# An MLP's up projection by Strassen's product in place of the plain product, in a hybrid encoder kernel on one core

## The chip, the core and the metric

The kernel runs on one core of one Trainium2 chip. The metric is the time of one execution on the device in microseconds (us); the time before is the median of three runs, 2505.2 us (2502.43 to 2505.82). The profile is that of one further execution.

The engines are named as in the profile: PE is TensorE (matmuls), PEld its weight load, DVE VectorE, ACT ScalarE, POOL GpSimd, SP SyncE, which here only issues DMAs. PSUM holds the sums of the matmuls; SBUF holds everything else.

## The reference

One layer of an encoder on 1024 tokens of width 1024, in float32: a mixer (windowed attention beside a Mamba-2 scan), cross-attention, an MLP, and a final norm. The change concerns the last three lines.

```python
D_MODEL = 1024
D_FF = 4 * D_MODEL
...
        x = x + merged @ w_out[i]
        h = rmsnorm(x, norm_cross[i])
        x = x + cross_attention(h, rmsnorm(mem, norm_mem[i]), w_xq[i], w_xkv[i], w_xo[i])
        h = rmsnorm(x, norm_ffn[i])
        x = x + jnp.square(jax.nn.relu(h @ w_up[i])) @ w_down[i]
    return rmsnorm(x, norm_final)
```

## The kernel before

**Number format.** Every matmul operand is split into two parts, hi (a rounded copy, made by ACT, L66) and lo (the rest, a subtraction on POOL or DVE, L67), and a product is three matmuls, hi·hi, hi·lo and lo·hi, in one PSUM bank (mm3, L79 to L86). A weight block of 128×1024 is loaded by SP into one of two buffers `raw`, split by wload into `whi` and `wlo` (three buffers each) and then used.

**The stages.** Input projections, Mamba and windowed attention come first; they are not touched but for the buffers' names. merge_cross_phase then makes the mixer's output, adds it to x (eight tiles x1 of 128 tokens by 1024, kept in SBUF), does cross-attention for two halves of 512 tokens, h = 0 and 1, and adds its output projection in 4 units a half (xo_units, PSUM tile `xops`, 48 matmuls of 256 columns each, and four additions on DVE). Among the last units stand the norms of the MLP's input: ACT sums the squares, DVE and POOL make the factor `rr` (L118, L120), DVE scales the row tile to `xn` (L135), PE transposes it (PSUM tile `nt`), and ACT and DVE split it into the tiles `kt` (h3T).

**The MLP** (mlp_phase, from L918) runs in 16 blocks of 256 hidden columns, with up one block ahead of down. Up: two weight blocks, each giving 128 hidden columns for 1024 tokens; 8 tiles of the inner dimension × 2 halves × 3 matmuls a block, in PSUM tile `ups`; then relu on ACT (L936), a product on DVE (L938), the split on ACT and DVE (L940, L941), the result `u` staying in SBUF. Down: two blocks of w_down (`wdh`, `wdl`); for each of the 8 token tiles and 2 column halves 6 matmuls into `dps` and an addition to x1 on DVE (L964). In the last block each token tile is normed and stored as soon as it is complete.

**What sets the order.** A scheduler arranges each engine's instructions from the program's order and the pools' buffers; what stands in an engine's queue is then taken in that order, each with its waits. DMAs of weights stand in SP's queue.

## Time and profile before

| | |
|---|---|
| median of 3 runs | 2505.2 us |
| profiled execution, its own time | 2506.1 us |
| its span (first to last instruction) | 2504.2 us |
| mean granted clock of TensorE | 0.994 |
| first matmul of the output units of half 1 | 1767.2 us |
| up projection, first matmul | 1794.7 us |
| last matmul | 2495.9 us |

The busy times of the engines are shares of the span. A row of a view by operation and tile gives the engine, the operation, out<-in by the program's names, the count, and durations in ns (minimum, median, maximum); a row of the grouped view gives the busy us and the mean ns. A timeline's row gives the start and the duration in us, and in square brackets the idle time of the engine before it with what ended it. PE's matmuls overlap, so that the time between two of them, not the duration of one, says what a matmul costs.

### The profile page before, as it was taken

To read this page: it belongs to the slowest core of one execution; us is meant where nothing else is said; L and a number is where in the kernel's file an instruction comes from. 1 tells how busy PE (TensorE), PEld (TensorE's weight loads), DVE (VectorE), ACT (ScalarE), POOL (GpSimd) and SP (SyncE) were. 2 spreads that over 40 slices of the span, in tenths; PEclk is the share of its full clock that TensorE was granted. 3 is DMA by queue.
4 is the path that set the end of the run, shared out by engine and by line. 5 is a ranking of instruction groups with operands and counts; after the bars stand their busy time and mean duration, and the time that the engine had idled before them with its cause. 6 is when DMAs were issued, how large, how long until landed. Compare 5 with 4: busy or idle time off the path is not lost.

```text
span 2504.2 us, 32169 instructions
## 1 busy us (share of the span) xinstructions
PE 2434.0 (97%) x12348; PEld 2023.8 (81%) x12348; DVE 1284.3 (51%) x2033; ACT 1025.3 (41%) x2114; POOL 935.5 (37%) x808
## 2 busy tenths in 40 slices
PE   7899999999999999999999999999999999999998
PEld 6688887878878788777777878888988888888887
DVE  5747656576665753665553343235544334343435
ACT  5436455463544643666772332235422121212112
POOL 5334526354363542454444344134331221213120
PEclk9999999999999999999999999999999999999999
DMA  6213223142232322111144453321221110101111
GB/s 224 92 55 116 70 83 114 59 131 60 93 101 68 118 64 72 45 49 37 48 141 154 171 189 127 144 76 51 76 76 43 49 53 34 68 34 62 39 34 67
DMA packets 135912, 212.19 MB, mean 85 GB/s; under 512 B 9680, under 2 KB 84560, under 8 KB 135760
## 3 DMA queue, kind: packets, MB, share of 16 engines
q1 hardware_dynamic: 64864, 171.34, 19.9%
q10 hardware_dynamic: 70896, 38.81, 5.5%
q8 instruction: 97, 1.59, 0.3%
q14 instruction: 55, 0.45, 0.1%
HBM read 183.63 MB, written 26.48 MB: 84 GB/s over the span
## 4 chain that ended last, share of the span: by engine, by line
PE 68%; DVE 12%; POOL 7%; ACT 6%; issue 4%; DMA 2%; SPq 0%; POOLq 0%; ACTq 0%; DVEq 0%
PE ups L81 5%; PE ups L86 5%; PE ups L85 5%; PE dps L86 4%; PE dps L85 4%; PE dps L81 4%; PE mps L85 3%; PE mps L86 3%; PE mps L81 3%; PE zp L86 2%; PE zp L85 2%; PE zp L81 2%; PE st L454 2%; POOL wlo L67 2%; DVE cx L342 2%
## 5 line engine op out<-in xcount | busy, mean ns | idle before, releaser
L67 POOL TENSOR_TENSOR wlo<-raw,whi 128x1024 fp32r<-128x1024 f32 x170 | 412.7, 2429 | 447.5 <-ACT whi L66 412.5
L66 ACT ACTIVATE whi<-raw 128x1024 fp32r<-128x1024 f32 x172 | 181.8, 1057 | 362.4 <-PE mps L85 118.5
L964 DVE TENSOR_TENSOR x<-x,dps 128x512 f32<-128x512 f32 x256 | 175.7, 687 | 124.7 <-PE dps L86 123.0
L67 POOL TENSOR_TENSOR wdl<-raw,wdh 128x1024 fp32r<-128x1024 f32 x32 | 76.0, 2396 | 423.2 <-ACT wdh L66 423.2
L81 PE MATMUL cps<-kt,whi 128*128 128x512 f32 x512 | 217.4, 425 | 8.8 <-DVE cx L342 8.8
L86 PE MATMUL cps<-kt,wlo 128*128 128x512 f32 x512 | 201.5, 394 | 0.0
L85 PE MATMUL cps<-kt,whi 128*128 128x512 f32 x512 | 200.8, 392 | 0.0
L81 PE MATMUL ups<-kt,whi 128*128 128x512 f32 x512 | 199.7, 390 | 0.0
L85 PE MATMUL ups<-kt,whi 128*128 128x512 f32 x512 | 199.4, 389 | 0.0
L86 PE MATMUL ups<-kt,wlo 128*128 128x512 f32 x512 | 199.2, 389 | 0.0
L81 PE MATMUL dps<-wdh,u 128*128 128x512 f32 x512 | 199.2, 389 | 0.0
L85 PE MATMUL dps<-wdl,u 128*128 128x512 f32 x512 | 199.2, 389 | 0.0
L86 PE MATMUL dps<-wdh,u 128*128 128x512 f32 x512 | 199.2, 389 | 0.0
L938 DVE TENSOR_TENSOR u<-ups,ru 128x512 f32<-128x512 f32 x64 | 44.2, 690 | 256.4 <-ACT ru L936 254.6
L66 ACT ACTIVATE wdh<-raw 128x1024 fp32r<-128x1024 f32 x32 | 32.3, 1053 | 229.9 <-PE dps L86 229.7
L81 PEld LDWEIGHTS cps<-kt,whi 128*128 128x128 f32 x512 | 97.5, 190 | 34.8 <-issue 16.1
L85 PEld LDWEIGHTS cps<-kt,whi 128*128 128x128 f32 x512 | 97.3, 190 | 26.3 <-issue 7.3
L468 POOL TENSOR_TENSOR cb_t<-prev,dec 128x256 f32<-128x256 f32 x48 | 32.7, 681 | 223.7 <-ACT prev L462 221.2
L86 PEld LDWEIGHTS cps<-kt,wlo 128*128 128x128 f32 x512 | 96.9, 189 | 21.0
L81 PEld LDWEIGHTS ups<-kt,whi 128*128 128x128 f32 x512 | 96.1, 188 | 20.5 <-DVE u L938 0.4
L85 PEld LDWEIGHTS ups<-kt,whi 128*128 128x128 f32 x512 | 96.1, 188 | 20.0 <-DVE kt L144 0.2
L81 PEld LDWEIGHTS dps<-wdh,u 128*128 128x128 f32 x512 | 96.1, 188 | 19.9
(312 smaller groups left out, 6527.4 us busy)
## 6 DMA issues: line engine op xcount, KB each, us to landing
rows<-d_cs ACTq DMA_DIRECT2D x128, 256.0 KB, 3.8
raw<-in_wssd_dram SPq DMA_DIRECT2D x48, 512.0 KB, 3.3
raw<-in_wsb_dram SPq DMA_DIRECT2D x32, 512.0 KB, 3.2
raw<-in_wup_dram SPq DMA_DIRECT2D x32, 512.0 KB, 3.1
raw<-in_wdn_dram SPq DMA_DIRECT2D x32, 512.0 KB, 3.2
x<-in_x_dram SPq DMA_DIRECT2D x16, 512.0 KB, 7.3
raw<-in_wg_dram SPq DMA_DIRECT2D x16, 512.0 KB, 3.8
d_y<-yts SPq DMA_DIRECT2D x32, 256.0 KB, 2.3
```

Source lines behind the costliest of these rows:

```text
L66: nc.scalar.activation(hi, raw, AF.Copy)
L67: (eng or nc.gpsimd).tensor_tensor(lo, raw, hi.bitcast(F32), ALU.subtract)
L81: i = mm(out, l[0], r[0], start=first, stop=False)
L85: mm(out, l[0], r[1], start=False, stop=False)
L86: mm(out, l[1], r[0], start=False, stop=last)
L342: V.scalar_tensor_tensor(acc[:, :S - o], ps[:, o:], cw(k), acc[:, :S - o], ALU.mult, ALU.add)
L454: PE.matmul(st[:, lo:hi], q.btok[:, c], xs.rearrange("p d h q -> p (d h q)")[:, lo:hi], start=True, stop=True)
L468: G.tensor_tensor(heads(t), heads(prev[:, c, 1]), decay(q, 1, c), ALU.mult)
L938: V.tensor_tensor(u2, pv, r, ALU.mult)
L964: V.tensor_tensor(xh, xh, ps, ALU.add)
```

## The change

Up is split in pairs of blocks, and each pair is computed by Strassen's product (in Winograd's form): with the inputs as a 2×2 matrix of halves (a11, a12 for the first 512 tokens, the two halves of the inner dimension; a21, a22 for the last), and a pair's weights as a 2×2 matrix b11, b12, b21, b22 of 512 columns each (two weight blocks), 7 products of 12 matmuls replace 8. Sums of the inputs are made once (`Up.sums`: s1 to s4 and a22, after the transposes of the last four norms), sums of the weights for each pair (`weights`: four differences on DVE, and seven operands `wop`, hi on ACT and lo on POOL, L1073 and L1074; six buffers `wop`, now shared with wload, and `raw` still two).

Products 1 and 2 need only a11 and a12, not the sums. For pairs 0 to 7 they are made **ahead**, between the output units of half 1 and the sums, and the results (x = product 1, and c11) stored in DRAM. Then come pairs 8 to 15 in full, and pairs 0 to 7 with the other five products and x loaded again. All results go to DRAM (`d_u`), and down runs after up, in 8 blocks of twelve matmuls per addition (L1215), loading u and w_down blocks; the first block is loaded under the last three pairs. The x1 tiles of the first half are parked in DRAM (`d_x`) during up and loaded again (`xl`) at down's start. The output units of half 1 are done in two passes (two token tiles each), so their weights are loaded and split twice. PE's order is the program's own in up and down.

```diff
 def wload(kx, src, n=1024, hi=None, lo=None, eng=None):
     if hi is None:
-        hi = kx.wp.tile([P, 1024], F32R, tag="whi", bufs=kx.w_bufs, name="whi")[:, :n]
-        lo = kx.wp.tile([P, 1024], F32R, tag="wlo", bufs=kx.w_bufs, name="wlo")[:, :n]
+        hi = kx.wp.tile([P, 1024], F32R, tag="wop", bufs=6, name="whi")[:, :n]
+        lo = kx.wp.tile([P, 1024], F32R, tag="wop", bufs=6, name="wlo")[:, :n]
     split_in(kx, src, hi, lo, eng)
     return hi, lo
...
+        kx.h3 = act_tiles(kx)
+        for i in range(2):
+            norm(0, i, g_ffn, [kx.h3])
+        for i in range(2, 4):
             values(i, pend[4 + i], oks[1])
-        kx.h3T = [act_tiles(kx)]
-        for i in range(4):
-            xo_units(1, oks[1], i)
...
-def mlp_phase(kx, ins, out):
...
+def xo_units(kx, ins, h, ok, c, js=range(4)):
...
+def up_phase(kx, ins, dr, ok, grow, x1_low):
...
+        for c in range(4):
+            xo_units(kx, ins, 1, ok, c, (0, 1))
+            park(c)
+            if c in (1, 2):
+                norm_split(kx, xns[c - 1], [a11, a12], (c + 1) * P)
+        x1_low.close()
+        with tc.tile_pool(name="tp", bufs=1, side="right", reuse_waits="tile") as tp:
+            up = Up(kx, ins, dr, mp, tp, {"a11": a11, "a12": a12}, grow)
+            xns = [rows(4), rows(5)]
+            up.ahead((0,))
+            xo_units(kx, ins, 1, ok, 0, (2, 3))
+            up.sums(0, xns[0])
+            xo_units(kx, ins, 1, ok, 1, (2, 3))
+            up.ahead((1,))
+            up.sums(1, xns[1])
+            for c in range(2, 4):
+                xo_units(kx, ins, 1, ok, c, (2, 3))
+            xns = [rows(6), rows(7)]
+            up.ahead((2, 3))
+            up.sums(2, xns[0])
+            up.ahead((4, 5))
+            up.sums(3, xns[1])
+            up.ahead((6, 7))
+            order = [b for b in range(16) if b not in up.early] + sorted(up.early)
+            w = up.weights(order[0])
+            for n, b in enumerate(order):
+                nxt = up.weights(order[n + 1]) if n < 15 else None
+                if n == 13:
+                    us = down_us(kx)
+                    for j in range(4):
+                        raw = mp.tile([P, D], F32, tag="ld", bufs=2, name="uraw")
+                        split_u(kx, dr, us, j, raw)
+                if n == 14:
+                    wd = [down_wd(kx)]
+                    for j in range(2):
+                        raw = mp.tile([P, D], F32, tag="ld", bufs=2, name="draw")
+                        split_wd(kx, ins, wd[0][2 * j:2 * j + 2], j, raw, nc.vector)
+                up.quad(b, w)
+                w = nxt
+            wd.append(down_wd(kx))
+            for j in range(2, 4):
+                raw = mp.tile([P, D], F32, tag="ld", bufs=2, name="draw")
+                split_wd(kx, ins, wd[1][2 * j - 4:2 * j - 2], j, raw, nc.vector if j == 2 else nc.gpsimd)
+    return us, wd[0] + wd[1]
+
+
...
+def split_u(kx, dr, us, m, raw):
+    nc = kx.nc
...
+        t = us[2 * (m % 4) + h]
+        rh = raw[:, h * 512:(h + 1) * 512]
+        nc.scalar.activation(t[:, 0], rh, AF.Copy)
+        nc.vector.tensor_tensor(t[:, 1], rh, t[:, 0].bitcast(F32), ALU.subtract)
+
...
+    nc.scalar.activation(hl[0], raw, AF.Copy)
...
+
...
+        s3["s2"] = kx.mp.tile([P, 4, 2, 512], F32R, tag="kt", bufs=4, name="kt")
+        for key in ("s1", "s3", "s4", "a22"):
+            s3[key] = mp.tile([P, 4, 2, 512], F32R, tag=key, bufs=1, name=key)
+        self.early = set()
...
+        return self.tp.tile([P, 512], F32, tag="t2", bufs=8, name=name)
...
+        def put(key, src, eng):
+            hi, lo = hl(key)
+            A.activation(hi, src, AF.Copy)
+            eng.tensor_tensor(lo, src, hi.bitcast(F32), ALU.subtract)
+
+        f1, f2, f3, f4 = (self.t2(n).rearrange("p (k c) -> p k c", k=4) for n in ("f1", "f2", "f3", "f4"))
+        h11, l11 = (x.bitcast(F32) for x in hl("a11"))
+        h12, l12 = (x.bitcast(F32) for x in hl("a12"))
+        A.activation(f1, pv[0], AF.Copy)
+        V.tensor_tensor(f3, h11, pv[0], ALU.subtract)
+        V.tensor_tensor(f1, f1, pv[1], ALU.add)
+        put("s1", f1, G)
+        V.tensor_tensor(f3, f3, l11, ALU.add)
+        V.tensor_tensor(f2, pv[1], f3, ALU.subtract)
+        put("s2", f2, G)
+        put("a22", pv[1], V)
+        put("s3", f3, G)
+        V.tensor_tensor(f4, h12, f2, ALU.subtract)
+        V.tensor_tensor(f4, f4, l12, ALU.add)
+        put("s4", f4, G)
+
+    def put(self, src):
+        t = self.kx.wp.tile([P, 2, 512], F32R, tag="wop", bufs=6, name="wop")
+        self.kx.nc.scalar.activation(t[:, 0], src, AF.Copy)
+        self.kx.nc.gpsimd.tensor_tensor(t[:, 1], src, t[:, 0].bitcast(F32), ALU.subtract)
+        return t
+
...
+    def weights(self, b):
+        V = self.kx.nc.vector
+        put = self.put
+        b11, b21 = self.raw(2 * b)
+        b12, b22 = self.raw(2 * b + 1)
+        ts = [self.t2(f"w{n}") for n in range(2)]
+        o = {} if b in self.early else {1: put(b11), 2: put(b21)}
+        V.tensor_tensor(ts[0], b12, b11, ALU.subtract)
+        V.tensor_tensor(ts[1], b22, ts[0], ALU.subtract)
+        o[6] = put(ts[1])
+        o[5] = put(ts[0])
+        V.tensor_tensor(ts[0], b22, b12, ALU.subtract)
+        o[7] = put(ts[0])
+        o[3] = put(b22)
+        V.tensor_tensor(ts[1], b21, ts[1], ALU.subtract)
+        o[4] = put(ts[1])
+        return o
+
+    def product(self, ps, w, n, start):
...
+        for k in range(4):
+            ks = slice(k * P, (k + 1) * P)
+            for m, (i, j) in enumerate(((0, 0), (0, 1), (1, 0))):
+                self.kx.nc.tensor.matmul(ps, w[:, i, ks], act[:, k, j], start=start and k == 0 and m == 0,
+                                         stop=k == 3 and m == 2, skip_group_check=True)
+
+    def square(self, c, b, j, h):
+        self.kx.nc.vector.scalar_tensor_tensor(c, c, 0.0, c, ALU.max, ALU.mult)
+        self.kx.nc.sync.dma_start(self.dr.u[2 * b + j][:, h * 512:(h + 1) * 512], c)
...
+    def ahead(self, bs):
+
+
+        kx = self.kx
+        for b in bs:
+            w = self.early_weights(b)
+            cd = kx.pg.tile([P, S], F32, tag="g", name="pcd")
+            x, c11 = self.t2("x"), self.t2("c11")
+            self.product(cd[:, :512], w[1], 1, True)
+            kx.nc.scalar.activation(x, cd[:, :512], AF.Copy)
+            kx.nc.sync.dma_start(self.dr.u[2 * b + 1][:, :512], x)
+            self.product(cd[:, 512:], w[2], 2, True)
+            kx.nc.vector.tensor_tensor(c11, x, cd[:, 512:], ALU.add)
+            self.square(c11, b, 0, 0)
+            self.early.add(b)
...
+    def quad(self, b, w):
+        kx = self.kx
+        V, A = kx.nc.vector, kx.nc.scalar
...
+        pb = kx.pp.tile([P, 512], F32, tag="p", name="pb")
+        cd = kx.pg.tile([P, S], F32, tag="g", name="pcd")
+        pc, pd = cd[:, :512], cd[:, 512:]
+        c12 = self.t2("c12")
+        if early:
+            x = self.t2("x")
+            kx.nc.sync.dma_start(x, self.dr.u[2 * b + 1][:, :512])
+        else:
+            c11 = self.t2("c11")
+            self.product(pb, w[1], 1, True)
+            A.activation(c11, pb, AF.Copy)
+            self.product(pd, w[2], 2, True)
+            V.tensor_tensor(c11, c11, pd, ALU.add)
+            self.square(c11, b, 0, 0)
+
+        def whole(dst, ps):
+            if early:
+                V.tensor_tensor(dst, x, ps, ALU.add)
+            else:
+                A.activation(dst, ps, AF.Copy)
+
+        self.product(pb, w[6], 6, early)
+        whole(c12, pb)
+        self.product(pc, w[5], 5, True)
+        c22, c21 = self.t2("c22"), self.t2("c21")
+        whole(c22, pc)
+        self.product(pb, w[7], 7, False)
+        V.tensor_tensor(c22, c22, pb, ALU.add)
+        self.square(c22, b, 1, 1)
+        self.product(pc, w[3], 3, False)
+        V.tensor_tensor(c12, c12, pc, ALU.add)
+        self.square(c12, b, 1, 0)
+        self.product(pb, w[4], 4, False)
+        if early:
+            V.tensor_tensor(c21, x, pb, ALU.add)
+            A.activation(c21, c21, AF.Relu)
+        else:
+            A.activation(c21, pb, AF.Relu)
+        A.activation(c21, c21, AF.Square)
+        kx.nc.sync.dma_start(self.dr.u[2 * b][:, 512:], c21)
...
+def down_phase(kx, ins, dr, first, out):
...
+        NB = 8
+
...
+                us, wd = down_us(kx), down_wd(kx) + down_wd(kx)
+            for j in range(4):
+                m = 4 * b + j
+                split_u(kx, dr, us, m, fp.tile([P, D], F32, tag="uraw", bufs=2, name="uraw"))
+                split_wd(kx, ins, wd[2 * j:2 * j + 2], m, kx.wp.tile([P, D], F32, tag="raw", bufs=2, name="raw"), G)
...
+        for t in range(4):
+            kx.x1[t] = xp.tile([P, D], F32, tag="xl", bufs=4, name="xl")
+            nc.sync.dma_start(kx.x1[t], dr.x1[t])
+        nxt = first
...
-                    for j in range(2):
-                        mm3(kx, ps, kt_pair(us[j][t // 4], slice((t % 4) * P, (t % 4) * P + P)),
-                            (wd[j][0][:, cs], wd[j][1][:, cs]), j == 0, j == 1)
+                    for j in range(4):
+                        mm3(kx, ps, kt_pair(us[2 * j + t // 4], slice((t % 4) * P, (t % 4) * P + P)),
+                            (wd[2 * j][:, cs], wd[2 * j + 1][:, cs]), j == 0, j == 3)
                     xh = kx.x1[t][:, cs]
                     V.tensor_tensor(xh, xh, ps, ALU.add)
```

POOL's queue at the end of the output units and the first sums. Before, it holds factors of norms (`rr`) and one lo part of a weight block (`wlo`) per block:

```order
L67 TENSOR_TENSOR wlo_16287<-raw_16288,whi_16286 128x1024
L120 TENSOR_TENSOR rr_16172<-rv_16170,mhalf_133 128x1
L67 TENSOR_TENSOR wlo_16356<-raw_16357,whi_16355 128x1024
L120 TENSOR_TENSOR rr_16196<-rv_16194,mhalf_133 128x1
L120 TENSOR_TENSOR rr_16218<-rv_16216,mhalf_133 128x1
```

In the changed kernel the same place of POOL's queue holds also the operands of the products made ahead (`wop`) and the lo parts of the sums (s1, s3, `kt` for s2, s4):

```order
L1074 TENSOR_TENSOR wop_16292<-raw_16290,wop_16292 128x512
L1074 TENSOR_TENSOR wop_16295<-raw_16290,wop_16295 128x512
L67 TENSOR_TENSOR wlo_16362<-raw_16363,whi_16361 128x1024
L1053 TENSOR_TENSOR s1_16131<-f1_16235,s1_16131 128x4x128
L1053 TENSOR_TENSOR s3_16132<-f3_16237,s3_16132 128x4x128
L67 TENSOR_TENSOR wlo_16396<-raw_16397,whi_16395 128x1024
L1053 TENSOR_TENSOR kt_16130<-f2_16236,kt_16130 128x4x128
L1053 TENSOR_TENSOR s4_16133<-f4_16238,s4_16133 128x4x128
```

One weight block's lo part now stands between four lo parts of sums, where before nothing but rr stood.

DVE's queue in the MLP. Before, in a steady block, it holds the up results (u2, u) between the additions of down:

```order
L938 TENSOR_TENSOR u2_17118<-ups_17067,ru_17116 128x512
L964 TENSOR_TENSOR x1_14262<-x1_14262,dps_17142 128x512
L941 TENSOR_TENSOR u_17120<-u2_17118,u_17120 128x512
L964 TENSOR_TENSOR x1_14262<-x1_14262,dps_17150 128x512
L938 TENSOR_TENSOR u2_17125<-ups_17067,ru_17123 128x512
```

In the changed kernel, in a pair whose products 1 and 2 were made ahead (c21 is the last result of the pair before; w0 and w1 are the differences for the pair after this one, c12 and c22 this pair's results; `pb` and `pcd` are PSUM):

```order
L1171 TENSOR_TENSOR c21_17916<-x_17888,pb_17885 128x512
L1089 TENSOR_TENSOR w0_17968<-raw_17966,raw_17964 128x512
L1090 TENSOR_TENSOR w1_17969<-raw_17966,w0_17968 128x512
L1096 TENSOR_TENSOR w1_17969<-raw_17964,w1_17969 128x512
L1093 TENSOR_TENSOR w0_17968<-raw_17966 128x512
L1154 TENSOR_TENSOR c12_17991<-x_17992,pb_17989 128x512
L1154 TENSOR_TENSOR c22_18019<-x_17992,pcd_17990 128x512
L1164 TENSOR_TENSOR c22_18019<-c22_18019,pb_17989 128x512
L1109 SCALAR_TENSOR_TENSOR c22_18019<-c22_18019 128x512
```

The four differences stand in one piece ahead of c12; L1096 and L1093 overwrite w1 and w0 and wait for POOL's lo parts that read them. PE runs products 6 (into `pb`), 5 (`pcd`), 7 (`pb`), 3 (`pcd`) and 4 (`pb`) of the pair.

SP's queue where up ends. Before, loads of weight blocks alternate to the end, two of each kind:

```order
L65 DMA raw_20330<-in_wup_dram 128x1024
L65 DMA raw_20399<-in_wup_dram 128x1024
L65 DMA raw_20468<-in_wdn_dram 128x1024
L65 DMA raw_20474<-in_wdn_dram 128x1024
L969 DMA out_0_dram<-xnf_20622 128x1024
```

In the changed kernel, where down begins:

```order
L1002 DMA uraw_18745<-d_u4_136 128x1024
L1002 DMA uraw_18755<-d_u5_137 128x1024
L1176 DMA d_u14_146<-c21_18654 128x512
L1012 DMA raw_18771<-in_wdn_dram 128x1024
L1002 DMA uraw_18765<-d_u6_138 128x1024
L1200 DMA xl_18719<-d_x0_128 128x1024
L1200 DMA xl_18721<-d_x1_129 128x1024
L1200 DMA xl_18723<-d_x2_130 128x1024
L1200 DMA xl_18725<-d_x3_131 128x1024
```

The reloads of x (`xl`) stand behind the loads of three u blocks of the second step, of which the third uses the first one's buffer again (two buffers `uraw`).

144 lines of the change are left out of this document (91 added, 53 removed).

## The prediction

> **What bounds the kernel now.** I read the head of the page first, then the chain of waits, then the stretch from the cross-attention's output units to the end, which is all that the change rewrites.
>
> ```profile
> span 2504.2 us, 32169 instructions
> PE 2434.0 (97%) x12348; PEld 2023.8 (81%) x12348; DVE 1284.3 (51%) x2033; ACT 1025.3 (41%) x2114; POOL 935.5 (37%) x808
> PE 68%; DVE 12%; POOL 7%; ACT 6%; issue 4%; DMA 2%; SPq 0%; POOLq 0%; ACTq 0%; DVEq 0%
> ```
>
> TensorE is busy 97% of the span, and the other engines at most 51%. The chain leads through PE for 68% only because earlier stages pass through softmax and state work. The table of busy time by stretch (us, then PE, weight load, DVE, ACT, POOL, each with its count, then clock, DMA share and GB/s) gives the stages touched: the output units of the second half, the start of the MLP, its steady state, and the end.
>
> ```profile
> 1767.20:1794.70 27.50, 27.50 (x234) 27.32 (x232) 15.95 (x32) 10.97 (x19) 11.75 (x7) 1.00 0.22 77
> 1794.70:1850.00 55.30, 54.36 (x249) 43.88 (x247) 27.49 (x36) 24.21 (x39) 20.75 (x11) 1.00 0.25 86
> 1900.00:2400.00 500.00, 500.00 (x2208) 414.15 (x2207) 189.20 (x272) 100.55 (x137) 112.87 (x48) 1.00 0.15 50
> 2480.00:2504.20 24.20, 16.23 (x72) 13.13 (x70) 18.57 (x28) 8.07 (x14) 3.85 (x7) 0.93 0.42 173
> ```
>
> In the MLP's steady state PE is busy 500 of 500 us at full granted clock, with DVE at 38%, ACT 20%, POOL 23%. There, work off PE is free and matmuls are the whole price. The additions of the down projection, each releasing six matmuls later, show what one matmul costs:
>
> ```profile
> 1900.59 0.69 DVE L964 TENSOR_TENSOR x<-x,dps 128x512 f32<-128x512 f32 x1 [0.67 <-PE dps L86]
> ...
> 1907.39 0.69 DVE L964 TENSOR_TENSOR x<-x,dps 128x512 f32<-128x512 f32 x1 [0.67 <-PE dps L86]
> L81 PE MATMUL ups<-kt,whi x512: 387/389/497, 1794.7 to 2451.9; 128*128 128x512 f32 x171
> 2495.85 0.39 PE L86 MATMUL dps<-wdh,u 128*128 128x512 f32 x1
> ```
>
> The first and last row stand five additions apart, 30 matmuls: 6.80/30 = 0.2267 us each (the 0.39 us durations overlap). Up and down together are 1536 + 1536 of them, 696.3 us; with some 3 us of transposes the MLP could take 699.2 us, and it took 701.4 (1794.7 to 2496.1). So only 2.2 us are lost there today.
>
> **The change part by part.**
>
> *Fewer matmuls.* Sixteen pairs at 7 products of 12 matmuls are 1344 instead of 1536; down keeps 1536 and the transposes stay. **192 × 0.2267 = 43.5 us** off PE. That is certain as long as PE has its operands; the rest of the sum is where it will not.
>
> The other engines are paid by these rows (by operation and tile):
>
> ```profile
> L964 DVE TENSOR_TENSOR x<-x,dps x256: 676/687/689, 1844.8 to 2496.4; 128x512 f32<-128x512 f32 x128
> L941 DVE TENSOR_TENSOR u<-u,u x64: 691/693/2477, 1816.8 to 2457.5; 128x512 fp32r<-128x512 f32 x64
> L940 ACT ACTIVATE u<-u 128x512 fp32r<-128x512 f32 x64 | 40.5, 632 | 73.1 <-DVE u L938 73.1
> L776 POOL TENSOR_TENSOR wo<-raw,wo 128x512 fp32r<-128x512 f32 x8 | 10.1, 1298 | 24.1 <-ACT wo L775 24.1
> L67 POOL TENSOR_TENSOR wlo<-raw,whi 128x1024 fp32r<-128x1024 f32 x170 | 412.7, 2429 | 447.5 <-ACT whi L66 412.5
> L135 DVE SCALAR_TENSOR_TENSOR xn<-x,rr,grow 128x1024 f32<-128x1024 f32 x11 | 14.1, 1285 | 7.8 <-POOL rr L120 7.8
> L120 POOL TENSOR_TENSOR rr<-rv,mhalf 128x1 f32<-128x1 f32 x18 | 9.9, 549 | 72.7 <-DVE rv L118 72.7
> ```
>
> So 0.69 us for a DVE operation of 512 columns, 0.63 on ACT, 1.30 on POOL (2.40 for 1024 where nothing disturbs it). One row stands out: L941, both inputs in SBUF, reaches 2477 ns, while L964, with one input in PSUM, never passes 689. The timeline shows why:
>
> ```profile
> 1813.89 4.81 POOL L67 TENSOR_TENSOR wlo<-raw,whi 128x1024 fp32r<-128x1024 f32 x2 [1.97 <-ACT whi L66]
> 1816.12 0.62 ACT L940 ACTIVATE u<-u 128x512 fp32r<-128x512 f32 x1
> 1816.77 2.47 DVE L941 TENSOR_TENSOR u<-u,u 128x512 fp32r<-128x512 f32 x1 [1.75 <-ACT u L940]
> 1819.35 0.69 DVE L938 TENSOR_TENSOR u<-ups,ru 128x512 f32<-128x512 f32 x1
> 1766.61 1.29 DVE L135 SCALAR_TENSOR_TENSOR xn<-x,rr,grow 128x1024 f32<-128x1024 f32 x1 [0.66 <-POOL rr L120]
> 1767.19 2.97 POOL L67 TENSOR_TENSOR wlo<-raw,whi 128x1024 fp32r<-128x1024 f32 x1 [0.61 <-ACT whi L66]
> ```
>
> The DVE operation of 1816.77 ends 0.54 us after POOL's pair (1818.70): it did its work only when POOL had finished. In the other direction POOL's 1767.19 took 2.97 instead of 2.40, having begun under a DVE operation that ended at 1767.90. I therefore add POOL's time and that of DVE operations with two SBUF inputs as if on one engine.
>
> *The transition* (xops of the second half, products made ahead, sums). PE has 27.5 us of xops (first row above), 192 matmuls made ahead (43.5 us) and the first two products of the first full pair (5.4): 76.4 us of cover. POOL must do in it 6 wxo lo parts × 2.40 = 14.4, 18 weight operands × 1.30 = 23.4, 16 lo parts of sums × 1.30 = 20.8, 6 rr × 0.55 = 3.3: 61.9. DVE operations of two SBUF inputs add 6 xn × 1.285, 8 squares × 0.69 and 12 sums × 0.69: 21.5. Together 83.4, 7 us more than the cover. PE's order is fixed here and each product waits for its own operand; small early waits (a norm that isn't ready, a raw block not landed) I put at 2.7, about one POOL operation. Less the 2.2 us that are lost there now: **+7.5 us**. Bounds: −2.2 (all overlaps) and, if 16 strided lo parts take what the nearest strided row takes, 16 × 0.97 more, +23:
>
> ```profile
> L227 POOL TENSOR_TENSOR wdt<-raw,wdt 128x512 fp32r<-128x512 f32 x1 | 2.3, 2268 | 0.0
> ```
>
> I take 1.30: a sum's lo part reads and writes runs of 128 columns, wdt's runs of 64 on a tile split finer, and the eight L776 rows stand nearer in form.
>
> *Full pairs (8).* 84 matmuls, 19.0 us. POOL: 7 × 1.30 = 9.1; DVE: ten operations, 6.9; ACT some ten, 6.3. All are under half of PE. Every PSUM hand-over has one product of 2.72 us between writer and reader's deadline against 0.6 to 0.7 us of reading: **0**. If that cover went, each late reading would cost 8 × its lateness.
>
> *Half-made pairs (8).* 60 matmuls, 13.6 us, five products P6, P5, P7, P3, P4. Here PE's third product accumulates into the bank pb that c12 (L1154) must read first. DVE's rows above put before c12: c21 of the pair before (needs its P4), then four weight differences for the pair after it, of which L1096 waits for POOL's lo part of operand 6 and L1093 for that of operand 5. From the end of P4: c21 0.69, w0 0.69, w1 0.69, hi 0.63, lo 1.30, then POOL goes straight on with the lo part of operand 5, 1.30, holding DVE off, L1096 0.69, L1093 0.69, c12 0.69: 7.4; eight hand-overs of 0.03 to 0.11 us (L940 to L941, and L941's end to L938, above) add 0.5. PE meanwhile has P6 and P5, 24 × 0.2267 = 5.4. The wait is 2.5 us. It occurs between pairs of this kind, six times (the last builds no weights, the first follows a full pair, 0.4): **+15.4 us**. Bounds: 0, where each DVE piece overlaps after all; 1.8 × 6 where DVE gets in between the two POOL operations.
>
> The Trainium skill, page "SBUF — State Buffer", section "SBUF: two separate sides", says that DVE (with two SBUF inputs) and a GpSimd operation that reads SBUF take a port pair as an exclusive lock for the whole instruction, and in "Who interferes with whom" that issue order decides who blocks. The trace agrees on the lock (2.47 us at 1816.77), and there DVE didn't get in between two POOL operations. By that rule the half-made wait is the 2.5 us; without a lock it would be 1.2 us, 7 in all.
>
> *Hand-over to down.* The first block's u and weights are loaded under the last pairs, but the parked rows of x (xl, four of 512 KB) stand on SP behind the third u block of the next step (uraw_18765 in the SP rows), which waits for DVE's lo parts of the first. Landing times:
>
> ```profile
> raw<-in_wup_dram SPq DMA_DIRECT2D x32, 512.0 KB, 3.1
> x<-in_x_dram SPq DMA_DIRECT2D x16, 512.0 KB, 7.3
> yk<-d_y SPq DMA_DIRECT2D x32, 256.0 KB, 5.7
> ```
>
> 3.1 for the u block, two ACT and two DVE pieces of it and of its neighbour, 4 to 5 us, then 3.1 to 7.3 for x: 10 to 15 us after the first product. Four PSUM buffers of twelve matmuls cover 10.9. **+2.5** (between 0 and 4.4).
>
> *Down* has half as many additions (twelve matmuls each), PE-bound as now. Tail: from the last matmul to the end of the norm and store, unchanged, 8 us. Before the transition PE's order is the same; some rows of DVE, ACT and POOL change places there: 0 ± 3.
>
> Sum: 2506.1 (the profiled execution, 1.9 over its span) − 43.5 + 7.5 + 0 + 15.4 + 2.5 = 2488.0. It lies 0.9 over the median shown, so **2487**.
>
> **The rivals.**
>
> *B, the half-made pairs don't wait.* P4's c21 and the differences may run earlier than I have them, as raw blocks often land in time. For: DVE has only 9 to 10 operations per 13.6 us. Against: the four differences do stand ahead of c12. It gives 2487 − 15 = 2472, and to 2464 with a transition fully covered.
>
> *C, strided POOL work.* At 2.27 us a sum's lo part: 2487 + 15.5 = 2502. For: the one strided row. Against: its finer pattern.
>
> *D, slower: the ring of two raw blocks.* A pair's two blocks are reloaded only after the last differences of the pair before, so a load's landing joins the chain in front of c12 once it takes longer than the 3.1 + 0.7 us it has. Half-made pairs move about 2.75 MB in 16 us (two blocks, x, three stores, the early down loads), 170 GB/s. Six loads at x's 7.3 instead of 3.8 add 21 us: 2508; from 7.7 us on it is slower by over 0.2%, and at 8.5 it is 2515. For: the 7.3 row, in a busy stretch. Against: the end of the span moves 173 GB/s (last stretch above), the wup blocks landed in 3.1 and PE's cover is two products.
>
> That the algorithm doesn't save matmuls is excluded: their count is fixed by the code.
>
> **How the numbers follow.** A 0.52 (2475 to 2500), B 0.20, C 0.14, D 0.14. The range goes from B's far end, 2464, to 2506, which takes in C and the lower part of D; about 0.12 of D is left out, with some 0.05 of odd cases. A measurement tells 0.2%, 5 us, from no change: 2500.2 to 2510.2. Faster: A, B and 0.04 of C, 0.76. Same: 0.10 of C and 0.03 of D, 0.13. Slower: 0.11.
>
> **What would show it.** Right: PE busy without gap in the eight full pairs, 19.0 us each; in half-made pairs a PE wait of 2 to 3 us ended by DVE L1154; in the transition PE waits ended by POOL's operands or sums' lo parts, 7 to 10 us; first dps additions waiting for xl. Wrong: half-made pairs of 13.6 us (B); POOL L1053 above 2 us (C); DVE L1089 ended by DMA raw with PE behind it (D); or a transition that begins more than 3 us from where its place in before would put it.

## The result, and the profile after

The changed kernel takes 2544.0 us (median of four runs), the kernel before, run beside it, 2505.5 us: a ratio of 1.0148 with an interval of 1.0124 to 1.0171, so it is **slower by 1.5%**, where 2487 us and faster had been forecast. (One of the four runs, at 6922 us, was in a slow state and is left out of the ratio; the median of the other three is 2541.4 us.) The profiled execution took 2546.5 us.

The head of the page after, the row of granted clock by slices, and the chain of waits:

```profile
span 2544.7 us, 32517 instructions
PE 2421.6 (95%) x12156; PEld 2002.4 (79%) x12156; DVE 1337.0 (53%) x2048; ACT 1072.0 (42%) x2214; POOL 1055.8 (41%) x905
PEclk9999999999999999999999999999989999999999
PE 62%; DVE 12%; POOL 8%; ACT 7%; issue 6%; DMA 4%; SPq 0%; ACTq 0%; POOLq 0%; DVEq 0%
```

The 192 matmuls are gone (12348 to 12156), but PE's busy time fell by only 12.4 us instead of 43.5: the matmuls that are left have become slower. And the span holds 123 us in which PE is not busy, where it held 70. The table by stretch (columns as before) shows where: the transition from the first output unit to the first full pair, the full pairs, the half-made pairs, and down.

```profile
1740.00:1876.55 136.55, 117.64 (x698) 102.44 (x699) 81.08 (x111) 58.69 (x97) 79.10 (x55) 0.94 0.34 114
1876.55:2046.10 169.55, 158.62 (x674) 126.76 (x673) 70.82 (x86) 56.48 (x97) 86.20 (x59) 0.98 0.31 103
2046.10:2185.60 139.50, 121.32 (x481) 95.43 (x480) 75.42 (x94) 40.83 (x64) 53.66 (x36) 0.93 0.43 146
2185.60:2537.00 351.40, 348.72 (x1537) 288.02 (x1535) 157.15 (x198) 68.72 (x99) 74.54 (x35) 1.00 0.28 98
```

The granted clock is 0.94 and 0.93 in the transition and in the half-made pairs; in the MLP of before it was 1.00. Against what the prediction's own steps give for the same stretches:

| stretch, us | PE's work alone | predicted | measured |
|---|---|---|---|
| start of the stretch (first output unit) | | 1734.0 | 1740.0 |
| transition (60.7 before, + 43.5 made ahead, + 2.9 transposes) | 107.1 | 116.8 | 136.6 |
| eight full pairs (672 matmuls) | 152.3 | 152.3 | 169.6 |
| eight half-made pairs (480) | 108.8 | 124.2 | 139.5 |
| down (1536) | 348.2 | 350.7 | 351.4 |

The four stretches are 53 us over the prediction, and the start is 6 us later; less half a us in the tail, these are the 58.5 us between 2488.0 and 2546.5, the profiled execution's time. The half-made pairs and down had a wait where I put it; the full pairs were to have none, and every stretch but down is longer than its waits explain.

The waits of PE in time order (rows of PE's timeline; start, duration, how many matmuls the row joins):

```profile
1812.53 4.55 PE L1105 MATMUL pcd<-kt,wop 128*128 128x512 f32 x12 [4.49 <-ACT x L1126]
1864.35 5.91 PE L1105 MATMUL pcd<-kt,wop 128*128 128x512 f32 x13 [3.32 <-ACT x L1126]
1887.57 2.93 PE L1105 MATMUL pb<-kt,wop 128*128 128x512 f32 x6 [5.41 <-ACT c L1147]
1953.97 3.06 PE L1105 MATMUL pcd<-s,wop 128*128 128x512 f32 x12 [0.79 <-DVE c L1149]
1956.86 2.96 PE L1105 MATMUL pb<-s,wop 128*128 128x512 f32 x12
2069.32 3.03 PE L1105 MATMUL pb<-s,wop 128*128 128x512 f32 x12 [2.50 <-ACT wop L1073]
2086.19 4.18 PE L1105 MATMUL pb<-s,wop 128*128 128x512 f32 x9 [2.70 <-ACT wop L1073]
2108.18 2.04 PE L1105 MATMUL pb<-s,wop 128*128 128x512 f32 x4 [5.07 <-DVE c L1154]
```

Four things are to be seen. (1) In the transition it is product 2 that waits, for ACT's copy x (L1126) of product 1, and in the full pairs product 5, for DVE's c11 (L1149) of product 2. Neither needs these results: they write the *other half* of the same PSUM tile `pcd`. (2) The first full pair's product 6 waits 5.41 us for ACT's c11 (L1147). (3) Behind some waits matmuls are slow: nine at 2086.19 take 4.18 us, where twelve at 2069.32 take 3.03. By the starts of the matmuls, 73 stand 0.427 us apart (33, 6 and 34 in the three stretches; in the MLP of before, none): 73 × 0.2 = 14.6 us. (4) Products that read s1, s3, s4 or a22 take 2.96 us a row where others take 2.88, wait or not.

How the waits add up, from the starts of the matmuls (stretches of over 0.6 us between two starts, less 0.227): 20.2 us in the transition, 12.2 in the full pairs, 19.7 in the half-made ones, 2.8 in down.

Why x is late at 1812: ACT's timeline, with DVE's and POOL's beside it.

```profile
1811.36 0.63 ACT L1052 ACTIVATE s<-f 128x512 fp32r<-128x512 f32 x1 [3.12 <-DVE f L1068]
1811.90 0.58 ACT L1126 ACTIVATE x<-pcd 128x512 f32<-128x512 f32 x1
```
```profile
1806.81 1.77 DVE L1067 TENSOR_TENSOR f<-kt,f 128x512 f32<-128x512 f32 x1
1808.61 2.71 DVE L1068 TENSOR_TENSOR f<-f,kt 128x512 f32<-128x512 f32 x1
```
```profile
1805.13 2.90 POOL L1053 TENSOR_TENSOR s<-f,s 128x512 fp32r<-128x512 f32 x2
1807.99 2.79 POOL L67 TENSOR_TENSOR wlo<-raw,whi 128x1024 fp32r<-128x1024 f32 x1
```

Product 1 had ended at 1808.0, but in ACT's queue the copy stands behind the hi part of s4, which waits for DVE's f4 (L1067, L1068), and these, 0.69 us each by themselves, take 1.77 and 2.71 beside POOL. So a sum that PE first reads at 1898.1, in the first full pair's product 3, holds PE 87 us earlier, through a queue and a shared PSUM tile. The lo parts of the sums cost 1.26 to 1.74 us, 1.44 in the mean: rival C did not come true.

Why c11 is late in a full pair, from DVE's timeline:

```profile
1950.92 0.69 DVE L1089 TENSOR_TENSOR w<-raw 128x512 f32<-128x512 f32 x1 [6.83 <-DMA raw<-in_wup_dram]
1951.65 1.67 DVE L1090 TENSOR_TENSOR w<-raw,w 128x512 f32<-128x512 f32 x1
1953.23 0.68 DVE L1149 TENSOR_TENSOR c<-c,pcd 128x512 f32<-128x512 f32 x1
```

c11 stands on DVE behind the first two differences of the next pair. In each of the eight full pairs the first of them waits 6.6 to 7.1 us for the next pair's raw block, so that c11 ends just before 1953.97, when product 5 starts.

And a half-made pair, which went as predicted but for the wait for a raw block, piece by piece (DVE and POOL):

```profile
2062.66 0.69 DVE L1089 TENSOR_TENSOR w<-raw 128x512 f32<-128x512 f32 x1 [0.65 <-DMA raw<-in_wup_dram]
2066.23 1.75 DVE L1096 TENSOR_TENSOR w<-raw,w 128x512 f32<-128x512 f32 x1 [2.16 <-POOL wop L1074]
2067.90 0.68 DVE L1093 TENSOR_TENSOR w<-raw 128x512 f32<-128x512 f32 x1
2068.50 0.67 DVE L1154 TENSOR_TENSOR c<-x,pb 128x512 f32<-128x512 f32 x1
```
```profile
2064.91 2.52 POOL L1074 TENSOR_TENSOR wop<-w,wop 128x512 fp32r<-128x512 f32 x2 [3.81 <-ACT wop L1073]
```

The differences, POOL's two lo parts in one go (2.52 us), L1096 held by the second of them (1.75 instead of 0.69), L1093, c12; PE goes on 0.15 us after c12's end. The page names ACT's wop for this wait because that piece ended last (2069.31), but it is an operand of the next pair; at 2108.18 the same wait is put down to DVE c L1154.

### The profile page after: what moved, and what is told of

Same layout as the page of the kernel before. It is cut to its first block, busy times and chain, and to the rows that moved or that the text cites. A ratio compares the mean times of both kernels' runs of the same rounds, so it can differ in the third digit from the quotient of the medians.

```text
span 2544.7 us, 32517 instructions
## 1 busy us (share of the span) xinstructions
PE 2421.6 (95%) x12156; PEld 2002.4 (79%) x12156; DVE 1337.0 (53%) x2048; ACT 1072.0 (42%) x2214; POOL 1055.8 (41%) x905
## 4 chain that ended last, share of the span: by engine, by line
PE 62%; DVE 12%; POOL 8%; ACT 7%; issue 6%; DMA 4%; SPq 0%; ACTq 0%; POOLq 0%; DVEq 0%
PE dps L81 4%; PE dps L85 4%; PE dps L86 4%; PE pcd L1105 4%; PE pb L1105 4%; PE mps L86 3%; PE mps L85 3%; PE mps L81 3%; PE zp L85 2%; PE zp L81 2%; PE zp L86 2%; DMA raw<-in_wup_dram 2%; PE st L462 2%; POOL prev L477 1%; DVE cx L350 1%
## 5 line engine op out<-in xcount | busy, mean ns | idle before, releaser
L67 POOL TENSOR_TENSOR wlo<-raw,whi 128x1024 fp32r<-128x1024 f32 x142 | 349.8, 2464 | 599.0 <-ACT whi L66 566.4
L1074 POOL TENSOR_TENSOR wop<-w,wop 128x512 fp32r<-128x512 f32 x64 | 92.1, 1445 | 117.6 <-ACT wop L1073 117.6
L81 PE MATMUL gps<-kt,whi 128*128 128x512 f32 x256 | 109.6, 428 | 0.0
L496 ACT ACTIVATE ef<-rows,ebias 128x128 f32<-128x128 f32 x256 | 83.2, 391 | 53.3 <-PE cb L511 49.6
L86 PE MATMUL mps<-yk,wlo 128*128 128x512 f32 x256 | 100.5, 393 | 4.8 <-POOL wlo L67 4.8
L680 POOL TENSOR_SCALAR t<-t,den 128x384 f32<-128x384 f32 (+1 forms) x128 | 69.2, 561 | 81.9 <-DVE den L678 73.7
L81 PE MATMUL dps<-kt 128*128 128x512 f32 x256 | 99.7, 390 | 2.7 <-DVE xl L1215 2.7
L86 PE MATMUL gps<-kt,wlo 128*128 128x512 f32 x256 | 101.8, 398 | 0.0
L1105 PE MATMUL pcd<-s,wop 128*128 128x512 f32 x384 | 95.9, 398 | 5.8 <-DVE c L1149 5.5
L85 PE MATMUL mps<-yk,whi 128*128 128x512 f32 x256 | 100.4, 392 | 0.8 <-DVE yk L734 0.8
L85 PE MATMUL gps<-kt,whi 128*128 128x512 f32 x256 | 101.2, 395 | 0.0
L81 PE MATMUL mps<-yk,whi 128*128 128x512 f32 x256 | 100.5, 393 | 0.0
L85 PE MATMUL dps<-kt 128*128 128x512 f32 x256 | 99.6, 389 | 0.0
L86 PE MATMUL dps<-kt 128*128 128x512 f32 x256 | 99.6, 389 | 0.0
```

Of the source, the lines that this page charges most:

```text
L67: (eng or nc.gpsimd).tensor_tensor(lo, raw, hi.bitcast(F32), ALU.subtract)
L81: i = mm(out, l[0], r[0], start=first, stop=False)
L85: mm(out, l[0], r[1], start=False, stop=False)
L86: mm(out, l[1], r[0], start=False, stop=last)
L496: A.activation(ef[:, h], rows[:, 0, h], AF.Exp, bias=kx.ebias[:, b, j, 0, o:o + 1])
L680: G.tensor_scalar(t4[:, i, :n], t4[:, i, :n], den[:, i:i + 1], 1.0, ALU.mult, ALU.mult)
```

## The experiments

Theories at this point: **(T1)** two halves of one PSUM tile count as one, so PE waits for a reading it doesn't need; **(T2)** DVE's order in the half-made pairs; **(T3)** a wait of PE halves its clock for the next matmuls; **(T4)** the start of s1, s3, s4, a22 (at 128 modulo 256 bytes of a partition, by the built program; kt tiles at 0) slows their products. The rival to all of them is the prediction's own view: POOL and the port it shares with DVE are simply full, and every wait removed comes back under another name. Each edit is on the changed kernel unless it says otherwise; times are medians, the ratio is to the kernel before, run beside them. The kernel before had medians from 2505.1 to 2511.3 us in the different sets of runs, so across sets it is the ratios that can be compared, and the us only to some 5 us. Waits are counted from the starts of the matmuls, as above; a row's bracket gives 0.1 to 0.2 us less.

**e1, a PSUM tile for product 2.**

```diff
-            self.product(cd[:, 512:], w[2], 2, True)
-            kx.nc.vector.tensor_tensor(c11, x, cd[:, 512:], ALU.add)
+            p2 = kx.pp.tile([P, 512], F32, tag="p", name="pd")
+            self.product(p2, w[2], 2, True)
+            kx.nc.vector.tensor_tensor(c11, x, p2, ALU.add)
...
+            pd = kx.pp.tile([P, 512], F32, tag="p", name="pd")
             self.product(pd, w[2], 2, True)
```

> Edit: product 2 gets a PSUM tile of its own (in the pairs made ahead and in the full pairs) instead of the second half of pcd. Theory 1 (PE waits because two halves of one PSUM tile count as one: product 2 waits for ACT's copy x, L1126, of product 1, product 5 waits for DVE's c11, L1149): all waits of PE ended by L1126 and L1149 go, 20.2 us (some of it the norms' waits) and 6.8 us, and with them the stretches of matmuls spaced 0.427 us in the transition; 2544 falls by 20 to 33 us, to 2511 to 2524. Rival (POOL's and the shared port's work is the limit of the transition, 83 us against 76 of cover): the waits come back under other names (operands, sums), and the gain is below 12 us.

Measured: 2518.5 us, ratio 1.0040 (1.0025 to 1.0055), some 27 us less by the two ratios. Product 2 now follows product 1 without a gap:

```profile
1804.55 2.91 PE L1105 MATMUL pcd<-kt,wop 128*128 128x512 f32 x12
1807.30 2.89 PE L1105 MATMUL pd<-kt,wop 128*128 128x512 f32 x12
```
```profile
1738.10:1855.30 117.20, 111.55 (x699) 100.39 (x700) 80.86 (x111) 58.17 (x97) 81.29 (x54) 0.97 0.39 129
1855.30:2018.00 162.70, 156.69 (x674) 127.30 (x673) 72.48 (x86) 56.50 (x97) 87.26 (x61) 0.98 0.33 111
```

The transition is 19 us shorter though POOL is as busy in it as before (81.29 us against 79.10): T1 holds, the rival falls here. All waits for ACT's x and DVE's c11 are gone; the first full pair's product 6 still waits for ACT's c11, now 6.2 us.

**e2, 128 bytes of padding.**

```diff
+        mp.tile([P, 32], F32, tag="pad", bufs=1, name="pad")
         for key in ("s1", "s3", "s4", "a22"):
```

> Edit: an unused tile of 128 bytes per partition ahead of s1, s3, s4 and a22, which moves them from 128 to 0 modulo 256 bytes; nothing else. Theory (the start of the moving operand sets the 0.233 us spacing of their products, against 0.2267 of the products that read kt tiles): 64 products x 12 matmuls go from 0.233 to 0.2267, 4.9 us less, 2544 to 2539; the alternation 0.229/0.238 disappears. Rival (the spacing is an after-effect of the stall ahead of these products, or of what the other engines do then): spacing and time as before the edit.

Measured: 2544.2 us, ratio 1.0138 (1.0116 to 1.0160): too near 1.0148 for the times to tell. The profile does tell. The same products (7, 3 and 4 of a full pair) now take 2.88 us a row, start to start 2.72 instead of 2.80:

```profile
1953.78 2.88 PE L1106 MATMUL pb<-s,wop 128*128 128x512 f32 x12
1956.50 2.88 PE L1106 MATMUL pcd<-s,wop 128*128 128x512 f32 x12
1959.22 2.88 PE L1106 MATMUL pb<-a,wop 128*128 128x512 f32 x12
```

So T4 holds by the spacing, 64 products × 0.08 = 5 us, but no gain in time is shown: part of it is lost at once, because PE then only comes earlier to the same waits: the wait for L1149 grew by 0.1 to 0.2 us a pair.

**e3, c12 ahead of the differences.**

```diff
         whole(c22, pc)
+        nxt = self.weights(then) if then is not None else None
         self.product(pb, w[7], 7, False)
```

> Edit: in the half-made pairs the next pair's weights (loads, differences, operands) are written behind the readings c12 and c22 of this pair, so that on DVE c12 stands ahead of the four differences. Theory of the prediction (c12 is late because it queues behind differences that wait for POOL): PE's waits ahead of product 7, measured 2.1 to 5.2 us and 17.8 us in six pairs, go; so do the matmuls at 0.427 us behind them, 31 x 0.2 = 6 us; 2544 falls by 18 to 24 us, to 2520 to 2526. Rival (the ring of two raw blocks or POOL is the limit of these pairs): the wait moves to products 6 or 5 of the next pair, whose operands are now made later, and the gain is below 6 us.

Measured: 2540.5 us, ratio 1.0125 (1.0102 to 1.0147), the half-made stretch 131.7 us. A miss, with a gain as small as the rival's: 15.2 of the 19.7 us of waits stayed, not ahead of products 6 or 5, as the rival had it, but ahead of product 7, and the releaser is one that I had not on the list:

```profile
2065.83 0.68 DVE L1173 TENSOR_TENSOR c<-x,pb 128x512 f32<-128x512 f32 x1
2072.87 0.69 DVE L1155 TENSOR_TENSOR c<-x,pb 128x512 f32<-128x512 f32 x1 [6.37 <-DMA x<-d_u]
```
```profile
2067.08 0.33 SPq L1080 DMA_DIRECT2D raw<-in_wup_dram  x1
2067.51 0.38 SPq L1111 DMA_DIRECT2D d_u<-c  x1
2067.98 0.38 SPq L1144 DMA_DIRECT2D x<-d_u  x1
```

c12 now waits for the reload of x. On SP that stands behind a raw load which waited for its buffer until 2067.08, and it landed 4.8 us after its issue. One late link had hidden the next.

**e5, the same with x reloaded one pair ahead** (two buffers of its own, the ring t2 one smaller).

```diff
+        if then in self.early:
+            self.x = self.tp.tile([P, 512], F32, tag="xe", bufs=2, name="x")
+            kx.nc.sync.dma_start(self.x, self.dr.u[2 * then + 1][:, :512])
```

> Edit on the changed kernel: as in e3 (c12 and c22 ahead of the next pair's four weight differences on DVE), and the reload of x for the next half-made pair is issued one pair ahead, into two buffers of its own (the ring t2 has 7 instead of 8). Theory (two links hold c12: the differences ahead of it on DVE, and, with those gone, the reload of x, which in e3 stood on SP behind a weight load that waited for a buffer and landed 5.2 us after product 5 began): PE's waits ahead of product 7 go, the half-made stretch falls from 139.5 us (131.7 in e3) to 110 to 117, and the time to 2514 to 2524. Rival (POOL and the two raw blocks are the limit in these pairs): waits move to products 6, 5 or 4, and the stretch stays above 125.

Measured: 2526.5 us, ratio 1.0068 (1.0053 to 1.0084); the stretch fell to 121.1 us, short of the 110 to 117 expected. T2 holds with x as its second link: of 19.7 us of waits 7.0 are left, all in one pair (1.4 us ahead of its product 7, and 5.6 us ahead of its product 4, put down to ACT wop).

**e4, work in the place of the wait.**

```diff
         whole(c22, pc)
+        if early:
+            spare = kx.pp.tile([P, 512], F32, tag="p", name="spare")
+            self.product(spare, w[5], 5, True)
         self.product(pb, w[7], 7, False)
```

> Edit: in the eight half-made pairs PE does 12 matmuls more, between products 5 and 7, into a PSUM tile that nothing reads (a repeated product 5): 96 matmuls, 22 us of added PE work. Theory of the clock (an idle stretch of PE of 2 us and more can halve the granted clock for the 7 to 14 matmuls behind it: 0.427 us instead of 0.227): the added work fills the wait, no matmul of these pairs is spaced 0.427 any more, and the time falls by 0 to 6 us although PE has more to do. Rival (the slow matmuls have another cause, such as DMA or port traffic of these pairs): they stay, and the time rises by 4 to 10 us.

Measured: 2548.7 us, ratio 1.0155 (1.0127 to 1.0183). The half-made stretch grew by 4.5 us, to 144.0, with 21.8 us more work in it; waits in it fell from 19.7 to 7.4 us and matmuls at 0.427 from 34 to 11. The time lies in the rival's range and the spacing speaks for T3: my expectation had overlooked that the added work also fills pairs which hardly waited. (The added work less the waits and slow matmuls saved is 21.8 − 12.3 − 4.6 = 4.9 us.) Alone it decides nothing.

**e10, waits made on purpose, first try** (on the kernel before: DVE writes an unused tile ahead of an addition of down).

> Edit on the kernel before: in each of the 16 blocks of down, ahead of one addition, DVE writes a tile that nothing reads, 6 times in the first two blocks, 7 in the next two, up to 13 in the last two, 0.69 us each, which holds one PSUM buffer and so PE, for about 1 to 5 us more from block to block. Theory of the clock: no matmul at 0.427 us behind waits of under 2 us, 7 to 14 of them behind waits of 3.4 us and more, and sometimes behind those of 2 to 3.4 us. Rival (slow matmuls belong to the traffic of Strassen's pairs): spacing 0.2267 behind every wait.

It took 2523.9 us in one run and gave no answer: the matmuls of up stand between those of down in PE's queue, and the longest wait of PE behind these additions was 1.6 us. Most of the added time is the last block's DVE work: the stretch behind the last matmul grew from 8.0 to 17.4 us.

**e12, waits made on purpose, second try** (on e9, below; in down, where nothing of Strassen's runs).

```diff
+                    if t in (2, 6) and ch == 0 and b < NB - 1:
+                        idle = fp.tile([P, 512], F32, tag="idle", bufs=1, name="idle")
+                        for _ in range(2 + b):
+                            V.tensor_tensor(idle, xh, ps, ALU.add)
+                        held = kx.pg.tile([P, S], F32, tag="g", name="held")
+                        PE.transpose(held[:, :P], idle[:, :P], kx.ident)
                     V.tensor_tensor(xh, xh, ps, ALU.add)
```

> Edit on e9: in each of down's first seven blocks, twice, DVE writes a tile that no result needs, 2 times in the first block, one more per block, 8 times in the seventh (0.69 us each), and PE makes one transpose of it before it goes on, so that PE waits some 1.5 to 6 us, twice each length, where no product of Strassen's and no sums are near. Theory of the clock: behind waits under 2 us all matmuls at 0.2267; behind every wait of 3.4 us and more 6 to 14 matmuls at 0.427; in between sometimes. Added time about 53 us of waits and 10 to 25 us of slow matmuls. Rival (the slow matmuls belong to the traffic of Strassen's pairs): none behind any of the 14 waits.

One run, 2570.4 us beside 2505.1. Its profile has fourteen such waits, from 1.7 to 6.1 us. Behind the four of 1.67 and 2.48 us no matmul stands 0.427 us from the next (0.22 to 0.24, the first 0.31); behind each of the ten of 3.2 us and more, 5 to 12 do. The timeline of PE behind one of each kind:

```profile
2223.53 0.30 PE L1231 MATMUL held<-ident,idle 128*128 128x128 f32 x1 [2.31 <-DVE idle L1229]
...
2224.13 0.40 PE L86 MATMUL dps<-wd,u 128*128 128x512 f32 x1
2224.36 0.40 PE L81 MATMUL dps<-wd,u 128*128 128x512 f32 x1
```
```profile
2248.67 0.30 PE L1231 MATMUL held<-ident,idle 128*128 128x128 f32 x1 [3.03 <-DVE idle L1229]
...
2249.45 0.63 PE L86 MATMUL dps<-kt 128*128 128x512 f32 x1
2249.88 0.63 PE L81 MATMUL dps<-kt 128*128 128x512 f32 x1
...
2252.70 0.40 PE L85 MATMUL dps<-kt 128*128 128x512 f32 x1
```

The granted clock behind the two is 1.00 and 0.55 (columns as in the tables by stretch):

```profile
2223.50:2226.50 3.00, 2.97 (x14) 2.48 (x15) 0.60 (x1) 0.00 (x0) 0.00 (x0) 1.00 0.00 0
2248.70:2252.40 3.70, 3.70 (x10) 2.95 (x11) 0.54 (x1) 0.00 (x0) 0.00 (x0) 0.55 0.02 4
```

T3 holds: the wait does it without any of Strassen's traffic. The Trainium skill, page "TensorE: Matmul & The Clock Gate", section "What's actually happening", gives half the clock after an idle window of about 3.4 us. Its section "Wait — 56ns, not 53.3ns?" gives 512 ÷ 1.2 GHz, 426.7 ns, from start to start of such matmuls in that state. The trace agrees on that spacing, 0.427 us; shorter waits than 3.4 us did it too (see the last section).

**e6, all repairs together** (e1; s1, s3, s4 and a22 allocated first, so that they start at 0 modulo 256; e5; the second full pair's weights written behind the first one's c11).

> Edits together: product 2 with a bank of its own (e1), s1, s3, s4 and a22 starting at 0 modulo 256 bytes (e2's effect, by allocating them first), the half-made pairs as in e5, and the second full pair's weights written behind the first one's products 1 and 2, so that ACT copies c11 before them (the wait of 5.4 us of PE ahead of the first product 6). If the losses found add up: transition 117 us, full pairs 152 to 155, half-made 110 to 117, down 352, with 1738 ahead and 8 behind: 2477 to 2489, that is 16 to 28 us below the kernel before. Rival (losses replace each other, since the port of DVE and POOL is what fills up once PE no longer waits): 2495 or more.

Measured: 2496.9 us, ratio **0.9954 (0.9939 to 0.9969)**: faster than the kernel before, but short of the 2477 to 2489 us expected, and in the rival's range.

```profile
1735.50:1850.60 115.10, 108.15 (x699) 97.58 (x700) 78.23 (x111) 58.09 (x97) 79.08 (x53) 1.00 0.40 133
1850.60:2012.10 161.50, 156.09 (x673) 127.69 (x672) 70.39 (x87) 56.40 (x98) 90.68 (x62) 0.98 0.34 112
2012.10:2132.40 120.30, 112.64 (x481) 91.25 (x480) 74.91 (x94) 39.28 (x64) 51.82 (x37) 0.97 0.49 165
```

The losses add up in the transition (115.1 us, clock 1.00 again), but not in the pairs: the first two full pairs and one half-made pair still wait, 3.3 us and 5.7 us at worst. So a part of the waits did come back under other names, as the rival has it, though not because POOL is full: it is busy 91 of the 161.5 us of the full pairs.

**e7, the buffers' names alone** (on the kernel before: six `wop` in place of three `whi` and three `wlo`).

> Edit on the kernel before: only the buffers' names of the weight blocks, six shared buffers wop for whi and wlo in place of three each; all else as before. Theory (this shift of the buffers alone makes the 6 us by which the changed kernel is later at 1734 us: 2.3 us at the first projections, 3.5 us in the merge): 2508 to 2512. Rival (run to run scatter of that stretch): within 2 us of before.

Measured: 2512.8 us, ratio 1.0017 (1.0008 to 1.0025), some 4 us. Up to the first output unit its queues stand in the order of the changed kernel's, since the name also moves instructions of DVE, ACT and POOL there. Its profile has that unit at 1740.4 us; but so has e10's, whose instructions up to there stand in the order of before (1734.0 us). And six profiles in the changed kernel's order (after, e1 to e5) have it at 1735.8 to 1742.4. So that place scatters by 6 us from execution to execution, and only the ratio speaks for the theory, for a part of the 6 us.

**e8, no pair made ahead** (on e6).

> Edit on e6: no pair is made ahead; all 16 pairs are made in full after the sums. Theory (the pairs made ahead are worth their cover: without them PE waits for the four sums, each a chain of some 12 us from the transposes to the last lo part, of which the second pass of output units covers 14): slower than e6 by 12 to 25 us. Rival (half-made pairs cost more than the cover is worth even after e5's edits): equal to e6 or faster.

Measured: 2508.6 us, ratio 0.9998 (0.9987 to 1.0008), 12 us slower than e6, at the low end of what was expected. Making pairs ahead is worth its cover once the half-made pairs run well.

**e9, the old names back** (on e6; the operands take `whi` and `wlo` in turn).

> Edit on e6: the weight blocks have their two names back (whi and wlo, three buffers each), and the operands of the products take the two in turn, so that everything ahead of the MLP has the buffers of the kernel before. Theory (e7: the shared name costs some 4 us in the first projections and the merge): first output units back at 1734 us (1735.5 in e6's profile, 1740 in the changed kernel's), time 2490 to 2495, 12 to 18 us below the kernel before. Rival (what e7 shows is a matter of chance positions, not of the name): as e6, 2497.

Measured: 2494.8 us, ratio **0.9938 (0.9925 to 0.9950)**. The interval overlaps e6's, so the gain over e6 is not shown; it is the fastest kernel tried, 16.5 us below the kernel before.

**e11, down's early loads spread** (on e9, one u block a pair).

> Edit on e9: the early loads of down's first block are spread over four half-made pairs, one u block each, in place of four at once ahead of the sixth pair. Theory (the wait of 5.7 us of PE in e6 ahead of a product 4 comes from ACT, DVE and POOL doing eight splits of u at once, ahead of the next weights' operands): it goes, with its 10 matmuls at 0.427 us, 5 to 8 us less than e9. Rival (that wait is the ring of raw blocks): no change.

Measured: 2498.0 us, ratio 0.9954 (0.9939 to 0.9969). A miss: the same pair waits 5.75 us, in e9 5.2. So four u blocks at once are not what holds PE ahead of that product 4. The profile of e9 shows what stands there (ACT, DVE, and PE last):

```profile
2063.08 1.06 ACT L1015 ACTIVATE kt<-draw 128x1024 fp32r<-128x1024 f32 x1 [2.33 <-DMA draw<-in_wdn_dram]
2064.18 1.23 DVE L1016 TENSOR_TENSOR kt<-draw,kt 128x1024 fp32r<-128x1024 f32 x1 [0.17 <-ACT kt L1015]
2068.22 1.75 DVE L1099 TENSOR_TENSOR w<-raw,w 128x512 f32<-128x512 f32 x1
2069.90 0.67 DVE L1174 TENSOR_TENSOR c<-c,pb 128x512 f32<-128x512 f32 x1
2070.72 1.19 PE L1108 MATMUL pb<-a,wop 128*128 128x512 f32 x2 [5.03 <-ACT wop L1076]
```

Product 4 writes `pb`, which the addition to c22 (L1174) must have read, and PE goes on 0.15 us after its end, in e5, e6 and e11 too; the wop that the row names is the next pair's. On DVE that addition stands behind the next pair's differences, where e5's edit had put them, and among these stands the lo part of a block of w_down (L1016), for whose load ACT had waited. In e11 it stands there still. No run took it away, so this is read from the rows and not tested.

## Why the prediction was wrong

- **Fewer matmuls, −43.5 us**: right in count (192); as time it holds at 0.2267 us a matmul, and that rate did not hold throughout.
- **The transition, +7.5**: the step failed at "each product waits for its own operand". Product 2 waited for the reading of the other half of its PSUM tile, and that reading stood in ACT's queue behind the sums (17 of the 20.2 us of waits; e1 took them away). I had forecast waits that end with POOL's operands or lo parts; none of these 20.2 us did. The 33 slow matmuls add 6.6. With e1 the transition is 117.2 us beside the 116.8 predicted, which is luck and no proof of my sum of POOL's work: the waits that e1 leaves there, 5.5 us, end with operations of DVE. (POOL's 81.3 us there can't be set beside my 61.9, which begin later: in the kernel before, POOL is busy 10.2 us in the first 33 us of this stretch.)
- **Full pairs, 0**: "Every PSUM hand-over has one product of 2.72 us between writer and reader's deadline" failed. Between product 2 and product 5 lies one product as I said, but product 5 needed no such hand-over at all in my account, and the reading is not done 0.7 us after product 2: c11 stands on DVE behind two differences that wait for the next pair's raw block. Waits for L1149 of 0.95 to 1.1 us in six of the pairs, and in the first pair one of 0.4 us and one of 5.6 for ACT's c11, which queued behind the next pair's operands, make 12.2 us; the misaligned operands make about 2.5 more and six slow matmuls 1.2.
- **Half-made pairs, +15.4**: the mechanism was right, in order and places (2.5 us a pair predicted, 2.1 to 2.9 in five pairs, 5.2 in one; 19.7 us in all). That the size of one pair came out as well is in part luck. Where nothing else stands in the chain, PE waits 2.1 us (at 2144); in three pairs a wait of DVE for a raw block adds 0.3 to 0.65, and in one a lo part of u, ahead of c21, some 0.7. In the pair of 5.2 a block of w_down is split in the same chain, on ACT (L1013) and on DVE (L1014, 1.21 us). The row that I read for POOL going straight on did not show it: at 1816.77 the second POOL operation had already run for 0.47 us. The rows at 2064.91 and 2066.23 do. The term was too small by 4 us, and it lacked its after-effect: 34 matmuls at 0.427 us, 6.8 us.
- **The clock**: no term and no rival had it. I summed waits as if PE resumed at full speed. The slow matmuls cost 14.6 us in the whole change; e12 shows that a wait is enough for them.
- **Hand-over to down, +2.5**: measured 2.8 us, at the wait for xl. Down and the tail came out right.
- **The part ahead, 0 ± 3**: 6 us late in the profile; e7 assigns about 4 us to the shared buffer name by its ratio, and the rest can't be told from scatter. A shift of 3 us between two profiles, which I had named as a sign, is too small to be one.
- **Rivals**: B and C did not occur. D, the ring of two raw blocks, occurred in small and in a place that I had not given it. In the half-made pairs DVE waited for a raw block four times, 3.3 us in all, of D's 21. In the full pairs the late raw block is the link ahead of c11, and it reached PE only through the shared PSUM tile: with e1 these waits are gone though the ring is as before.

Of the 58.5 us of error, 19.8 lie in the transition, 17.3 in the full pairs, 15.3 in the half-made ones, 6 ahead of them. T1 is shown by e1, T4 by e2's spacing, T2 with its second link by e3 and e5, T3 by e12. The remaining wait ahead of a product 4 is read from rows alone (e11), and how much of the 6 us is the name's is open.

## What to carry to other kernels

When a tuned, PE-bound stage gets less matmul work, list for each product not only its operands but who must have read the *tile* it writes, all of it and not the half, and what stands ahead of that reader in its queue. Price a wait of PE at its length plus the slow matmuls behind it: behind waits of over 3 us these cost 1.0 to 2.6 us more here. And take a late link away together with the next one behind it: c12's queue hid a reload, and alignment's gain went into the next wait.

## What the runs showed of the hardware

- **The clock after a wait.** Over eleven profiles (after, e1 to e6, e8, e9, e11, e12), of PE's waits of 0.6 us and more from the output units on, ahead of 512-column matmuls, those of 3.2 us and more were followed by matmuls at 0.427 us in 42 of 43 cases (the one other was followed by a second wait at once), those of 2.1 to 3.0 us in 17 of 35, three in between in 1, and those below 2.1 us only in 4 of 93, each within 3 us of another wait. So between 2.1 and 3 us the length alone does not decide; what does was not tried. The Trainium skill, in the first section named above, wants a whole idle window of about 3.4 us, free-running, ahead of the slower clock. The runs differ, since 17 waits of at most 3.0 us did it.
- **The start of the moving operand.** A 512-column matmul of four-byte values took 0.227 us, by the median, where the tile began at 0 modulo 256 bytes, and 0.229 to 0.241, 0.233 in the mean, where it began at 128. Padding of 128 bytes brought these to 0.227 (e2); other starts were not tried.
- **A DVE operation beside POOL** took 1.77 and 2.71 us instead of 0.69, each ending some 0.54 us after the POOL operation beside it (1808.03 and 1810.78), and POOL's operations of 1.30 us took 1.45 in the mean over the 64 of L1074 on differences.
